# Bias steps as broadcast compares on VectorE, another order of the first operands, and three groups of transposes a chunk later

## The chip, the cores and the metric

The kernel runs on one core of a Trainium2 chip. The metric is the device time of one execution in microseconds (us). The engines are named as in the profile: PE (TensorE: matrix products and transposes), DVE (VectorE), ACT (ScalarE), POOL (GpSimd) and SP (SyncE, which here only issues DMAs).

## The reference

Two transformer blocks are computed one after the other for 256 tokens of width 2048, in float32.

The first block norms x, projects it to 13,712 columns (`proj = h @ w_in`), and runs three branches: A, sparse attention whose keys are the top 64 of an index score, with a learned bias per distance bucket (`bias = rel_table[t5_bucket(pq[:, :, None] - pk)]`); B, causal attention with low-rank q and k and rotary parts; and C, attention to 256 memory tokens (`mkv = rms_norm(mem) @ w_mem_kv`). Each branch's output is multiplied by silu of a z projection, goes through its matrix of `w_branch`, is gated by a sigmoid and added up, and `x = x + merged @ w_out`.

The second block norms this x (h2), projects to 8192 columns, runs a gated recurrence in two directions (its output is ho) and a short convolution, multiplies by `w_out_2`, norms again (h3), and ends with a gated feed-forward layer and a last norm.

## The kernel before, in words

**Tiling.** Each large matrix product is a Job: 512 columns of a weight, all rows of its depth. Its depth is cut into chunks of two tiles of 128 (KG = 2). A chunk's weights come by one DMA on SP (tile raw, 512 KB), ACT rounds them to wh (L277) and DVE takes the rest as wl (L278); the activations exist as such pairs too. `products` (L281) then issues twelve matmuls per chunk, for two token halves t: wh with the high part (L292), wh with the low part (L293), wl with the high part (L295). There are 764 chunks. `drive` (L297) goes through them: loads are issued up to seven chunks ahead, splits up to three ahead (fewer in the first twelve), then the products, the evacuation at a job's end, and one call of `side`.

**Side work.** Everything else is written as Python generators that yield a number of chunks to wait. `side` (L230) moves the urgent ones on each time, and the lanes (constants, bias, C, A, B, recurrence) in their order until the debt of ACT or DVE is above 1.6; each helper (`act`, `tt`, `ts`, ...) adds an estimate of its operation's time to its engine's debt, and each chunk takes a fixed amount off it. So the order on every engine is fixed when the program is built; each engine then works its queue in order and waits by semaphores. `force` (L247) runs side work until an event has come, when an evacuation needs it; no products lie between its rounds.

**Start.** `constants` issues the loads of the identity (on POOL's queue) and of mem's gains vr (on ACT's). `gen_in` loads mem: its first 512 columns in two halves ahead of the first weights. `begin` (L1065) runs some zero matmuls (`warm`), transposes the first tile of mem in two PSUM banks, transposes the gains (`gains0`), writes mem's first pair of columns as memh and meml, splits the first chunk, and writes the second pair.

**Bias.** `gen_bias` builds A's bias by distance: for each of six units u, `steps(u)` writes 0/1 rows stepm (positions compared with thresholds, ptile), eight matmuls with dbt sum the bucket differences, and a copy goes out to DRAM and back in another layout.

**Transposes.** An activation that feeds the next product is transposed on PE and split, by `gen_T`, some chunks after its evacuation: x after w_out and w_out_2 (`x_next`), ho (`g_evac` of block 2), and the q and k parts of B (`gen_B_half`: POOL norms them and applies rotation, tiles uq, bpe, bpt; two chunks or more later PE transposes).

Of the kernel before, what the change touches and what calls it, by code (L numbers as in the profile page):

```python
# [16 lines left out]
P = 128  # L17
# [9 lines left out]
KG = 2  # L27
# [3 lines left out]
WARM = 3  # L31
# [70 lines left out]
class Builder:  # L102
# [151 lines left out]
    def load_to(self, n):  # L254
        while self.nd < min(len(self.chunks), n):
            d = self.nd
            for f in self.pre.get(d, ()):
                f()
            j, _, ks, _, _ = self.chunks[d]
            r = self.praw.tile([P, KG, 512], F32, name="raw")[:, :len(ks), :j.n]  # L260
            w = j.w[ks[0] * P:(ks[-1] + 1) * P, j.n0:j.n0 + j.n].rearrange("(k p) n -> p k n", p=P)
            if d == 0:
                for k in range(len(ks)):
                    self.nc.sync.dma_start(r[:, k], w[:, k])
            else:
                self.nc.sync.dma_start(r, w)
            self.raws[d] = r
            self.nd += 1

    def split_to(self, n):  # L270
        while self.ns < min(len(self.chunks), n):
            j, _, ks, _, _ = self.chunks[self.ns]
            r = self.raws.pop(self.ns)
            wh = self.ph.tile([P, KG, 512], F32R, name="wh")[:, :len(ks), :j.n]
            wl = self.pl.tile([P, KG, 512], F32R, name="wl")[:, :len(ks), :j.n]
            for k in [slice(i, i + 1) for i in range(len(ks))] if self.ns == 0 else [slice(0, len(ks))]:
                self.nc.scalar.activation(wh[:, k], r[:, k], AF.Copy)  # L277
                self.nc.vector.tensor_tensor(wl[:, k], r[:, k], wh[:, k].bitcast(F32), op=ALU.subtract)  # L278
            self.whs[self.ns] = (wh, wl)
            self.ns += 1  # L280
# [46 lines left out]
    def gen_T(self, src, hi, lo, g=None, ev=None, free=(), nk=4, pause=False):  # L327

        banks = []
        for b in range(nk // 2):  # L330
            p = self.ps()
            for jj in range(2):
                for t in range(2):
                    self.tr(p[:, jj * 256 + t * P:jj * 256 + (t + 1) * P], src(t, 2 * b + jj))
            banks.append(p)
        yield 1
        for b, p in enumerate(banks):
            if b and pause:
                yield 1
            if g is None:  # L340
# [107 lines left out]
    def constants(self):  # L448
        nc, I = self.nc, self.I
        self.ident = self.const([P, P], "ident")  # L450
        nc.gpsimd.dma_start(self.ident, I["k_ident"])
        self.vr0 = self.slots.get([P, P], F32, "vr0")
        nc.scalar.dma_start(self.vr0[:16], I["mem_norm_g"][0].rearrange("(k p) -> k p", p=P))
# [140 lines left out]
    def warm(self):  # L594

        z = self.work([P, 512], "warm")
        self.nc.vector.memset(z, 0.0)
        p = self.ps()
        for _ in range(WARM):
            self.nc.tensor.matmul(p[:, :256], z[:, :P], z[:, :256], start=True, stop=True)  # L600
        y = self.work([P, 512], "warm")
        self.act(y[:, :8], z[:, :8], AF.Square)

# [6 lines left out]
    def gen_in(self, src, name, g0, r, hs, ls, at, every):  # L610
# [3 lines left out]
        def load(c):  # L614
            if c == 0 and at < 0:
                for h in range(2):
                    self.nc.sync.dma_start(tiles[0][:, :, h * 256:(h + 1) * 256], src[:, h * 256:(h + 1) * 256].rearrange("(b p) n -> p b n", p=P))
# [88 lines left out]
    def gen_bias(self):  # L706
# [8 lines left out]
        def steps(u):  # L715
# [3 lines left out]
            ms = [sl.get([P, 2, 512], F32R, "stepm") for _ in range(2)]  # L719
            for j in range(4):  # L720
                for i in range(ng):
                    g = 32 * tt + 4 * ((u - 2 * tt) * ng + i) + j
                    self.ts(ms[j // 2][:, j % 2, i * ns:(i + 1) * ns], self.posS[:, :ns], self.ptile[:, g:g + 1], None, ALU.is_le, eng="g")
# [235 lines left out]
    def gen_B_half(self, half, ct, sw, bc):  # L959
# [5 lines left out]
        for i in range(2):  # L965
# [16 lines left out]
            yield 3  # L982
# [69 lines left out]
    def block1(self):  # L1052
# [12 lines left out]
        def begin():  # L1065
            self.warm()
            next(gmem)
            self.gains0()
            next(gmem)
            self.split_to(1)  # L1070
# [188 lines left out]
    def x_next(self, x, cb, ssp, r, store, g, name):  # L1259
# [5 lines left out]
        def later():  # L1265
            yield 1
# [201 lines left out]
    def block2(self):  # L1468
# [45 lines left out]
        def g_evac(hf):  # L1514
            def evac(pts):
# [10 lines left out]
                def later():  # L1526
                    yield 1
# [189 lines left out]
```

## Time and profile before

| What | Value |
|---|---|
| Times of 3 runs | 2268.71, 2270.42 (median), 2270.98 us |
| Profiled execution, its own time | 2268.29 us |
| Its span in the trace | 2266.4 us |
| PE busy | 2243.3 us (99%) |
| Weight loads (PEld) busy | 1877.0 us (83%) |
| DVE busy | 1318.7 us (58%) |
| ACT busy | 1106.0 us (49%) |
| POOL busy | 368.8 us (16%) |
| Chain that ended last | PE 77%, issue 15%, POOL 1%, DMA 1% |
| Mean granted clock of PE | 0.997 |

The share of busy time says which engine the others work for; where time is lost is read from the waits of that engine and from its timeline. The end of a matmul is modelled in the trace, so the distance from one start to another start is the safer measure. A wait is put down to the engine whose semaphore came last.

### The profile page before, as it was taken

The page shows a single profiled execution, that of the slowest core. Times are in us where ns is not written, and L with a number is a line of the kernel's source. Part 1 is how long each engine was busy: PE and PEld are TensorE (multiplying, and loading weights), DVE is VectorE, ACT ScalarE, POOL GpSimd, SP SyncE. Part 2 cuts the span into 40 slices and gives each one's busy share as a digit, 9 for nine tenths or more (in the row PEclk, how much of TensorE's full clock was granted, in tenths as well). Part 3 has the DMA queues.
Part 4 walks back from the last instruction along what each step waited for, and adds up shares of the span by engine and source line. Part 5 has one row for each costly group of instructions (what it writes and reads, how often), then busy time and mean ns, then how long its engine had stood idle before and what let it go on. Part 6 is the DMA issues. An engine that isn't in the chain of part 4 may idle for free.

```text
span 2266.4 us, 27702 instructions
## 1 busy us (share of the span) xinstructions
PE 2243.3 (99%) x10514; PEld 1877.0 (83%) x10514; DVE 1318.7 (58%) x1460; ACT 1106.0 (49%) x1410; POOL 368.8 (16%) x299
## 2 busy tenths in 40 slices
PE   9989999999999999999999999999999999999998
PEld 7878888888888888878888888888888888888886
DVE  5744676655757555555676786555445444544545
ACT  5634545455555544444654655444444433444434
POOL 2093102201405110000363352000000000000001
PEclk9999999999999999999999999999999999999999
DMA  8545555545655556666655555555565566656564
GB/s 278 186 152 183 162 170 181 179 153 173 194 166 177 167 186 187 192 198 202 185 162 164 168 168 158 184 188 186 186 195 190 190 192 202 202 186 194 188 194 140
DMA packets 214933, 413.99 MB, mean 183 GB/s; under 512 B 13538, under 2 KB 20304, under 8 KB 214800
## 3 DMA queue, kind: packets, MB, share of 16 engines
q1 hardware_dynamic: 211936, 405.98, 56.5%
q0 software_dynamic: 2256, 5.19, 0.8%
q8 instruction: 82, 1.34, 0.2%
q10 hardware_dynamic: 608, 1.06, 0.1%
q14 instruction: 51, 0.42, 0.1%
HBM read 408.51 MB, written 3.67 MB: 182 GB/s over the span
## 4 chain that ended last, share of the span: by engine, by line
PE 77%; issue 15%; POOL 1%; DMA 1%; ACT 0%; DVE 0%; ACTq 0%; POOLq 0%; DVEq 0%; SPq 0%
PE acc L292 23%; PE acc L293 23%; PE acc L295 23%; PE sp L157 4%; PE sp L177 2%; DMA xres<-in_x_dram 0%; DMA gf<-in_final_norm_w_dram 0%; POOL x L132 0%; ACT wh L277 0%; POOL ho L132 0%; POOL bpt L132 0%; ACT x L128 0%; POOL bpe L132 0%; DVE wl L278 0%; POOL rs L201 0%
## 5 line engine op out<-in xcount | busy, mean ns | idle before, releaser
L278 DVE TENSOR_TENSOR wl<-raw,wh 128x1024 fp32r<-128x1024 f32 (+4 forms) x765 | 982.2, 1292 | 794.8 <-ACT wh L277 791.8
L277 ACT ACTIVATE wh<-raw 128x1024 fp32r<-128x1024 f32 (+4 forms) x765 | 800.6, 1053 | 868.2 <-PE acc L293 842.3
L292 PE MATMUL acc<-wh,xh 128*128 128x512 f32 (+2 forms) x864 | 341.6, 395 | 0.0
L293 PE MATMUL acc<-wh,xl 128*128 128x512 f32 (+2 forms) x864 | 337.1, 390 | 0.0
L292 PE MATMUL acc<-wh,h3h 128*128 128x512 f32 x704 | 274.8, 390 | 0.0
L293 PE MATMUL acc<-wh,h3l 128*128 128x512 f32 x704 | 273.9, 389 | 0.0
L295 PE MATMUL acc<-wl,xh 128*128 128x512 f32 (+2 forms) x864 | 229.9, 388 | 0.0
L292 PE MATMUL acc<-wh,h2h 128*128 128x512 f32 x512 | 202.2, 395 | 0.0
L293 PE MATMUL acc<-wh,h2l 128*128 128x512 f32 x512 | 199.4, 390 | 0.0
L295 PEld LDWEIGHTS acc<-wl,xh 128*128 128x128 f32 x864 | 162.2, 188 | 32.8
L293 PEld LDWEIGHTS acc<-wh,xl 128*128 128x128 f32 x864 | 163.5, 189 | 31.2
L292 PEld LDWEIGHTS acc<-wh,xh 128*128 128x128 f32 x864 | 163.5, 189 | 30.9
L295 PE MATMUL acc<-wl,h3h 128*128 128x512 f32 x704 | 188.2, 389 | 0.0
L295 PEld LDWEIGHTS acc<-wl,h3h 128*128 128x128 f32 x704 | 132.1, 188 | 27.5
L293 PEld LDWEIGHTS acc<-wh,h3l 128*128 128x128 f32 x704 | 132.2, 188 | 27.2
L292 PEld LDWEIGHTS acc<-wh,h3h 128*128 128x128 f32 x704 | 132.2, 188 | 27.1
L295 PE MATMUL acc<-wl,h2h 128*128 128x512 f32 x512 | 136.9, 389 | 0.0
L292 PE MATMUL acc<-wh,ah 128*128 128x512 f32 x344 | 134.0, 390 | 0.0
L293 PE MATMUL acc<-wh,al 128*128 128x512 f32 x344 | 133.8, 389 | 0.0
L295 PEld LDWEIGHTS acc<-wl,h2h 128*128 128x128 f32 x512 | 96.1, 188 | 20.0
L292 PEld LDWEIGHTS acc<-wh,h2h 128*128 128x128 f32 x512 | 96.2, 188 | 19.0
L293 PEld LDWEIGHTS acc<-wh,h2l 128*128 128x128 f32 x512 | 96.2, 188 | 18.9
(461 smaller groups left out, 2788.7 us busy)
## 6 DMA issues: line engine op xcount, KB each, us to landing
raw<-in_w_in_dram SPq DMA_DIRECT2D x328, 512.0 KB, 3.7
raw<-in_w_gate_up_dram SPq DMA_DIRECT2D x176, 512.0 KB, 3.7
raw<-in_w_down_dram SPq DMA_DIRECT2D x88, 512.0 KB, 3.9
raw<-in_w_out_dram SPq DMA_DIRECT2D x64, 512.0 KB, 4.1
raw<-in_w_branch_dram SPq DMA_DIRECT2D x48, 512.0 KB, 3.9
raw<-in_w_mem_kv_dram SPq DMA_DIRECT2D x31, 512.0 KB, 4.9
raw<-in_w_in_dram SPq DMA_DIRECT2D x8, 464.0 KB, 3.2
raw<-in_w_in_dram SPq DMA_DIRECT2D x8, 448.0 KB, 3.3
```

The source lines that it names most:

```text
L157: self.nc.tensor.matmul(out, lhsT, rhs, start=start, stop=stop)
L177: self.nc.tensor.transpose(out, in_, self.ident if k == P else self.ident[:k, :k])
L277: self.nc.scalar.activation(wh[:, k], r[:, k], AF.Copy)
L278: self.nc.vector.tensor_tensor(wl[:, k], r[:, k], wh[:, k].bitcast(F32), op=ALU.subtract)
L292: self.nc.tensor.matmul(outs[t], a, wh[:, kk], start=first and kk == 0, stop=False)
L293: self.nc.tensor.matmul(outs[t], b, wh[:, kk], start=False, stop=False)
L295: self.nc.tensor.matmul(outs[t], a, wl[:, kk], start=False, stop=last and kk == len(ks) - 1)
```

## The change

- The first operands: the identity is loaded by ACT's queue, vr by SP's, ahead of mem; the second half of mem's first tile is issued behind the first raw tile. There are four warm matmuls in the program in place of three, the gains are transposed first, and conversion of mem and split of the first chunk take turns (`split_first`). These splits now go through the helpers that add to the debt.
- `steps` makes four compares on DVE per unit, each over 512 columns, with positions and thresholds both broadcast, where POOL made 16 or 8 with one threshold each.
- The wait before the transposes is one chunk longer in `x_next` and for ho (`later`), and in `gen_B_half` for q's parts (`yield 4`).

```diff
@@ load_to
                 for k in range(len(ks)):
                     self.nc.sync.dma_start(r[:, k], w[:, k])
+                    if k == 0:
+                        self.second()
@@ new function
+    def split_first(self, k):
+
+        if k == 0:
+            self.whs[0] = (self.ph.tile([P, KG, 512], F32R, name="wh"), self.pl.tile([P, KG, 512], F32R, name="wl"))
+        r, (wh, wl) = self.raws[0], self.whs[0]
+        self.act(wh[:, k], r[:, k])
+        self.tt(wl[:, k], r[:, k], wh[:, k].bitcast(F32), ALU.subtract)
...
@@ gen_T
+            if pause:
+                yield 1
         yield 1
         for b, p in enumerate(banks):
-            if b and pause:
-                yield 1
-            if g is None:
+            if pause and b == 0:
+                for j in range(2):
+                    self.act(hi[:, j, :], p[:, j * 256:(j + 1) * 256], AF.Copy, scale=g(j))
+                    self.stt(lo[:, j, :], p[:, j * 256:(j + 1) * 256], g(j), hi[:, j, :].bitcast(F32), ALU.mult, ALU.subtract)
+                    yield 1
+            elif g is None:
@@ constants
-        nc.gpsimd.dma_start(self.ident, I["k_ident"])
+        nc.scalar.dma_start(self.ident, I["k_ident"])
...
-        nc.scalar.dma_start(self.vr0[:16], I["mem_norm_g"][0].rearrange("(k p) -> k p", p=P))
+        nc.sync.dma_start(self.vr0[:16], I["mem_norm_g"][0].rearrange("(k p) -> k p", p=P))
@@ gen_in
+                half(0)
+                self.second = lambda: half(1)
@@ gen_bias, steps
+            g0 = 32 * tt + 4 * (u - 2 * tt) * ng
+            thr = self.ptile[:, g0:g0 + 4 * ng].rearrange("p (i j) -> p j i", j=4)
+            pos = self.posS[:, :ns].unsqueeze(1).to_broadcast([P, ng, ns])
             for j in range(4):
-                for i in range(ng):
-                    g = 32 * tt + 4 * ((u - 2 * tt) * ng + i) + j
-                    self.ts(ms[j // 2][:, j % 2, i * ns:(i + 1) * ns], self.posS[:, :ns], self.ptile[:, g:g + 1], None, ALU.is_le, eng="g")
+                self.tt(ms[j // 2][:, j % 2, :].rearrange("p (i s) -> p i s", i=ng), pos,
+                        thr[:, j, :].unsqueeze(2).to_broadcast([P, ng, ns]), ALU.is_le)
@@ gen_B_half
             self.tt(pe, pe, tmp, ALU.add, "g")
-            yield 3
+            yield 4
@@ begin
             self.warm()
-            next(gmem)
             self.gains0()
             next(gmem)
-            self.split_to(1)
+            next(gmem)
+            next(gmem)
+            for k in range(KG):
+                next(gmem)
+                self.split_first(k)
@@ x_next, and g_evac of block 2
         def later():
-            yield 1
+            yield 2
```

**The start, on PE.** Before, the gains' transpose (vr) stands behind mem's eight:

```order
L1713 UNCONDITIONAL_BRANCH
L600 MATMUL sp<-warm 128x256 x3
L177 MATMUL sp<-ident,mem_102 128x128 x8
L606 MATMUL sp<-ident,vr_89 128x16
L292 MATMUL acc<-wh,memh_94 128x512
L293 MATMUL acc<-wh,meml_98 128x512
```

Now, in the same place:

```order
L1741 UNCONDITIONAL_BRANCH
L623 MATMUL sp<-warm 128x256 x4
L627 MATMUL sp<-ident,vr_89 128x16
L177 MATMUL sp<-ident,mem_102 128x128 x8
L304 MATMUL acc<-wh,memh_94 128x512
L305 MATMUL acc<-wh,meml_98 128x512
```

The products' order is as before; ahead of them the gains come first, and there is a warm matmul more.

**The bias steps.** Before, POOL's queue in the stretch of the first three units (rs is a power for a norm; ck and cq are branch C's k and q, normed there; biasd is the bias on its way through DRAM):

```order
L201 TENSOR_TENSOR r_83<-rs_t,cneg 128x2
L137 TENSOR_SCALAR stepm<-posS,ptile 128x128 x16
L201 TENSOR_TENSOR rs_1169<-rs_t,cneg 128x4
L132 TENSOR_TENSOR ck_403<-ck_403,rs_1169 128x512 x2
L137 TENSOR_SCALAR stepm<-posS,ptile 128x128 x16
L741 DMA biasd_1128<-bev 128x4x128
L137 TENSOR_SCALAR stepm<-posS,ptile 128x256 x8
L201 TENSOR_TENSOR rs_1382<-rs_t,cneg 128x4
L132 TENSOR_TENSOR cq_1287<-cq_1287,rs_1382 128x512 x2
```

Now DVE's queue in the same stretch, between the splits wl (bev is the copy of a unit's sums, ss a sum of squares):

```order
L290 TENSOR_TENSOR wl<-raw,wh 128x1024
L132 TENSOR_TENSOR stepm<-posS,ptile 128x512 x4
L290 TENSOR_TENSOR wl<-raw,wh 128x1024 x2
L146 TENSOR_REDUCE ss_705<-sq 128x2
L290 TENSOR_TENSOR wl<-raw,wh 128x1024
L137 TENSOR_SCALAR rs_t<-ss_705 128x4
L290 TENSOR_TENSOR wl<-raw,wh 128x1024
L137 TENSOR_SCALAR cq_1236<-acc,r_83 128x512
L132 TENSOR_TENSOR stepm<-posS,ptile 128x512 x4
L290 TENSOR_TENSOR wl<-raw,wh 128x1024 x2
L153 COPY bev<-sp 128x512
```

All six steps are gone from POOL; on DVE a split stands behind each group of four. Four or five splits lie from one group to the next.

**The end of branch B, on PE.** Before, a whole chunk lies between the last four transposes of prob and the six matmuls that use them and others (ukv holds B's values; the row with x6 holds two matmuls of one round and four of the next):

```order
L295 MATMUL acc<-wl,xh_110 128x512 x4
L157 MATMUL sp<-ukv_5142,pT 128x128 x4
L177 MATMUL sp<-ident,prob 128x128 x4
L292 MATMUL acc<-wh,xh_111 128x512
L293 MATMUL acc<-wh,xl_115 128x512
...
L295 MATMUL acc<-wl,xh_111 128x512 x4
L157 MATMUL sp<-ukv_5165,pT 128x128 x6
```

Now the last products ahead of them, and what follows:

```order
L305 MATMUL acc<-wh,xl_114 128x512
L307 MATMUL acc<-wl,xh_110 128x512 x4
L157 MATMUL sp<-ukv_5096,pT 128x128 x4
L177 MATMUL sp<-ident,prob 128x128 x4
L157 MATMUL sp<-ukv_5126,pT 128x128 x6
L304 MATMUL acc<-wh,xh_107 128x512
```

The transposes have moved next to the six matmuls, all of it in the forced rounds ahead of the evacuation of B's first z.

## Rows read from the trace of the kernel before

**Rows 1.** Waits of PE, then of its loads: us in total, times, longest.

```profile
PE sp L177 <- POOL cq L132: 3.1, 2, 2.4
PE sp L157 <- POOL stepm L137: 2.6, 2, 1.6
PE sp L177 <- POOL bpe L132: 1.7, 1, 1.7
PE acc L292 <- ACT wh L277: 1.7, 1, 1.7
...
PE sp L177 <- DVE x L132: 1.3, 3, 0.7
...
PEld sp L177 <- DVE x L132: 3.2, 6, 1.2
...
PEld sp L177 <- POOL ho L132: 0.7, 1, 0.7
```

**Rows 2.** Timeline of PE, 119 to 130: start, us, what.

```profile
118.97 0.39 PE L292 MATMUL acc<-wh,xh 128*128 128x512 f32 x1
...
119.88 1.08 PE L295 MATMUL acc<-wl,xh 128*128 128x512 f32 x4
...
129.20 1.09 PE L295 MATMUL acc<-wl,xh 128*128 128x512 f32 x4
```

**Rows 3.** Timeline of PE, 150 to 161.

```profile
151.04 1.07 PE L295 MATMUL acc<-wl,xh 128*128 128x512 f32 x4
...
159.76 1.09 PE L295 MATMUL acc<-wl,xh 128*128 128x512 f32 x4
```

**Rows 4.** Busy times in a stretch; PEclk is the granted clock.

```profile
125.50:128.50 3.00, 3.00 (x8) 2.32 (x8) 0.69 (x1) 0.00 (x0) 2.92 (x4) 0.50 0.04 14
```

**Rows 5.** Timelines of DVE and POOL, 126 to 160.

```profile
142.96 0.16 DVE L137 TENSOR_SCALAR rs_t<-ss 128x4 f32<-128x4 f32 x1
...
139.40 12.23 POOL L137 TENSOR_SCALAR stepm<-posS,ptile 128x256 fp32r<-128x256 f32 x8
151.60 1.03 POOL L201 TENSOR_TENSOR rs<-rs_t,cneg 128x4 f32<-128x4 f32 x1
152.71 2.74 POOL L132 TENSOR_TENSOR cq<-cq,rs 128x512 f32<-128x512 f32 x2
```

**Rows 6.** Timeline of PE around undisturbed transposes of mem, and the first of x.

```profile
25.45 1.07 PE L295 MATMUL acc<-wl,memh 128*128 128x512 f32 x4
...
27.16 0.47 PE L292 MATMUL acc<-wh,memh 128*128 128x512 f32 x1
...
968.87 1.07 PE L295 MATMUL acc<-wl,mgh 128*128 128x512 f32 x4
...
972.01 0.48 PE L292 MATMUL acc<-wh,mgh 128*128 128x512 f32 x1
```

**Rows 7.** DVE groups by shape: busy us, mean ns, idle before.

```profile
L278 DVE TENSOR_TENSOR wl<-raw,wh 128x1024 fp32r<-128x1024 f32 x52 | 64.5, 1246 | 43.3 <-ACT wh L277 42.6 <-PE acc L293 0.3 <-PE sp L177 0.2
...
L132 DVE TENSOR_TENSOR ctmp<-posS,k 128x256 f32<-128x256 f32 x1 | 0.4, 419 | 0.0
...
L132 DVE TENSOR_TENSOR nkb<-hK,nkb 128x1024 f32<-128x1024 f32 x2 | 6.2, 3092 | 0.0
```

**Rows 8.** Timeline of ACT at the end of branch B.

```profile
783.69 0.58 ACT L128 ACTIVATE pT<-sp 128x512 f32<-128x512 f32 x1
```

**Rows 9.** Timeline of PE at the start.

```profile
1.48 2.93 PE L600 MATMUL sp<-warm 128*128 128x256 f32 x6 [1.48 <-DVE warm L597]
...
9.15 0.79 PE L292 MATMUL acc<-wh,memh 128*128 128x512 f32 x1 [1.66 <-ACT wh L277]
...
12.73 1.12 PE L295 MATMUL acc<-wl,memh 128*128 128x512 f32 x4
```

**Rows 10.** DMA issues in the first 16 us: KB each, median us to landing.

```profile
mem<-in_mem_dram SPq DMA_DIRECT2D x2, 256.0 KB, 3.4
...
vr<-in_mem_norm_g_dram ACTq DMA_DIRECT2D x1, 8.0 KB, 2.5
```

More of the change, by code (lines that the diff above doesn't have):

```diff
@@ L30 @@
 NSLOT = 31
-WARM = 3
+WARM = 4
 T2 = 5
@@ L268, in load_to @@
             self.nd += 1
+    def split_first(self, k):
[4 more added lines that the diff above has]
+        self.tt(wl[:, k], r[:, k], wh[:, k].bitcast(F32), ALU.subtract)
+        if k == KG - 1:
+            del self.raws[0]
+            self.ns = 1
     def split_to(self, n):
@@ L275, in split_to @@
             wl = self.pl.tile([P, KG, 512], F32R, name="wl")[:, :len(ks), :j.n]
-            for k in [slice(i, i + 1) for i in range(len(ks))] if self.ns == 0 else [slice(0, len(ks))]:
-                self.nc.scalar.activation(wh[:, k], r[:, k], AF.Copy)
-                self.nc.vector.tensor_tensor(wl[:, k], r[:, k], wh[:, k].bitcast(F32), op=ALU.subtract)
+            self.nc.scalar.activation(wh, r, AF.Copy)
+            self.nc.vector.tensor_tensor(wl, r, wh.bitcast(F32), op=ALU.subtract)
             self.whs[self.ns] = (wh, wl)
@@ L597, in warm, with busy @@
         self.nc.vector.memset(z, 0.0)
-        p = self.ps()
-        for _ in range(WARM):
-            self.nc.tensor.matmul(p[:, :256], z[:, :P], z[:, :256], start=True, stop=True)
+        self.zero = z
+        self.busy(WARM)
         y = self.work([P, 512], "warm")
         self.act(y[:, :8], z[:, :8], AF.Square)
+    def busy(self, n):
+        p = self.ps()
+        for _ in range(n):
+            self.nc.tensor.matmul(p[:, :256], self.zero[:, :P], self.zero[:, :256], start=True, stop=True)
     def gains0(self):
@@ L615, in load @@
             if c == 0 and at < 0:
-                for h in range(2):
-                    self.nc.sync.dma_start(tiles[0][:, :, h * 256:(h + 1) * 256], src[:, h * 256:(h + 1) * 256].rearrange("(b p) n -> p b n", p=P))
+                half = lambda h: self.nc.sync.dma_start(tiles[0][:, :, h * 256:(h + 1) * 256],
+                                                        src[:, h * 256:(h + 1) * 256].rearrange("(b p) n -> p b n", p=P))
+                half(0)
+                self.second = lambda: half(1)
                 self.done(f"{name}L{c}")
@@ L1526, in later @@
                 def later():
-                    yield 1
+                    yield 2
                     yield from self.gen_T(lambda t, j: o[:, t, j * P:(j + 1) * P], h, l, g=lambda j: self.vT[:, c + j:c + j + 1],
```

## The prediction

> **What bounds the kernel now.** I read the busy table first, the one that stands in the section on the profile: TensorE (PE) is busy for 99% of the span, so only what makes PE stand still, or run slowly, can move the time. So I took the list of PE's waits next. Five of its eight entries make 10.4 us, and each is at a place that this diff touches [rows 1]. Their true cost is larger than the list says, since a matmul's end is modelled and since a stop lowers the clock, so I measured each in the timeline of PE, as the distance between two rows against what the work between them takes undisturbed. Products of 512 columns stand 0.227 us apart: from 118.97 to 119.88 there are four [rows 2]. Four products and eight transposes behind them, up to the next chunk, take 27.16 - 25.45 = 1.71 us, so eight transposes are 0.80 [rows 6]. A chunk is twelve products, 2.72 us; its weights are split on ScalarE and DVE up to three chunks ahead.
>
> **Bias steps from GpSimd to VectorE.** Before, POOL computes 64 step rows. Between the last products of two chunks at 119.88 and 129.20 lie twelve products and eight stepm matmuls, 20 x 0.227 = 4.54 us, and 9.32 are spent: 4.78 lost, partly in waits for POOL's stepm, partly because the granted clock in 125.5 to 128.5 is 0.50, the 1.2 GHz level, after PE had stood [rows 2, 4]. The stop at cq is of the same origin: VectorE (DVE) has written the sums at 142.96, but POOL is in a run of eight compares of 12.23 us until 151.60; only then come the power (1.03) and the two products (2.74) for which PE's transposes wait [rows 5]. From 151.04 to 159.76 are 8.72 us against 2.72 + 0.80 = 3.52: 5.20 lost [rows 3]. Without compares POOL can start 8.5 us earlier, and the wait of cq is 3.1: this stop goes whole.
>
> What is added are 24 tensor_tensor on DVE, 128x512, in six steps of four. The trace has no compare of two tensors on DVE. A 128x256 product with a broadcast operand takes 0.419, so two are 0.84; half a split of 128x1024 is 0.62; and the worst product in SBUF of the whole run, nkb, took 3.09 for 1024, 1.55 per 512 [rows 7]. I take 0.70, near the first two: 2.8 us per step and 16.8 in all. PE needs a step four or more chunks (10.9 us) after it is issued, so the matmuls find it done. What stands behind the compares on DVE are the splits (wl) that PE needs; they run three chunks ahead, 8.2 us, and a step with one split takes 2.8 + 1.25 = 4.05 [rows 7]. Cost on PE: nothing, and if that cover were gone, up to the 16.8. I count 4.8 + 5.2 = 10.0 gained.
>
> The planner counts the compares as DVE work and holds branch C back for them, by some ten chunks in the order; C is still done when z of c asks for it, and no row of PE is moved next to one that it waits for, so this is counted at nothing.
>
> **One chunk later.** The stop at bpe is 1.7 [rows 1]; the chunk added (2.72 x 384 / 512 = 2.0 for the narrower products there) is longer, so it goes: 1.7. The transposes of x after w_out wait for DVE's add, which itself waited for the residual's load. The first lost 972.01 - 968.87 = 3.14 against 1.71, so 1.43 [rows 6]. For all x and ho the list of weight loads says 3.2 + 0.7 = 3.9, as an upper bound; the 1.43 alone is the lower one. I take 3.0, nearer to the loads' list, because it counts more places than the first. What is late next: h2's and h3's last group is ready two chunks into a job that first uses it in its seventh chunk, so nobody.
>
> The same delay has a price at the end of branch B. There the evacuation of z forces B to its end, with no products between. Before, four transposes of prob had a whole chunk of cover before their copy was used; now they stand directly ahead of the six pT matmuls, four of which need ScalarE's copy of them. That copy took 0.58 [rows 8]; a little for the handover is added and the two matmuls that don't need it are taken off. Bounds: 0 if records pipeline well, 3.2 if PE stands 1.5 and loses the clock as in rows 2 (eight products at twice 0.227 cost another 1.8, less what overlaps). Taken: 0.6 lost.
>
> **The start.** PE's warm matmuls begin at 1.48 and six took 2.93; then it waits for the identity that POOL's queue loads, transposes at half rate, waits again (1.66) for the first split, and begins products at 9.15 [rows 9]. Eight products then take 12.73 - 9.15 = 3.58 us, 0.45 each, the 1.2 GHz level, before it runs at 0.227. In the new order the identity goes out on ScalarE's queue, where the 8 KB gains took 2.5 us from issue to landing, and the gains on SP ahead of the first half of mem (256 KB, 3.4) [rows 10]. The row of warm matmuls gets two instructions longer and, at 0.45 each, ends at about 1.48 + 8 x 0.45 = 5.1; the identity (0.72 + 2.5, with a margin for eight times the bytes) is there by then. The first half of mem, issued half a microsecond later than now, lands at about 1.2 + 3.4 = 4.6; four transposes (0.80, twice what four take at full rate) behind the gains' end at 6.1. The second half of mem now stands behind a raw block: issued near 2.2, it lands 3.4 to 4.2 later, up to 6.4, and its transposes end by 7.2, while ScalarE converts and splits the first k. First product at about 7.3: 1.85 earlier, bounds 0 (all loads later) and 2.5. As PE now works from 1.48 almost without a gap, the clock should rise before the products, which is worth 3.58 - 8 x 0.227 = 1.76 more; against this, the second block's conversion and split on ScalarE and DVE will be asked for earlier than they can be, which I estimate at 1 us. Together 1.85 + 1.76 - 1.1 = 2.5, bounds 0 and 3.6.
>
> The Trainium skill (TensorE: Matmul & The Clock Gate, Part 4: PE-mode transpose) speaks against the clock's share: it says that transposes do not count as busy time for the clock gate. By this rule the transposes between the warm matmuls and the products would leave the clock low, which is the first rival below. The trace of before cannot decide it, as its transposes there have stops on both sides.
>
> **Sum.** 10.0 + 1.7 + 3.0 - 0.6 + 2.5 = 16.6 us. The profiled execution took 2268.29, so 2251.7 for such a one; its time lies 2.1 us below the median 2270.42 of the timed runs, so I forecast 2270.4 - 16.6 = 2253.8.
>
> **Rivals.**
> *The clock stays low through the first products* (the transposes don't raise it). For it: after six warm matmuls and eight transposes the products of before still began at half rate; against it: PE stood still twice in between, which it would not now. The 1.76 goes, and of the 1.1 against it only about 0.85 stays, since loads of the second block are then asked for later: the start gives 1.85 - 0.85 = 1.0 in place of 2.5: 2255.3. 20%.
> *The forced end of B costs the clock too*: the order stands for it, the smallness of a 0.58 copy against it. 3.2 in place of 0.6: 2256.4. 8%.
> *Compares as slow as nkb*, 1.55 each: a step is 6.2, and in the five chunks (13.6 us) between steps stand five splits (6.2) and some 2.5 of other work: 14.9, so 1.3 late each time, 7.8 for six steps: 2261.6. For it: nkb has SBUF on both sides like the compares; against it: the other rows of this shape are at 0.42 per 256. 8%.
> *Slower: the step holds back the splits until PE stops and the clock falls.* Place: each of the six steps on DVE. Price: 4.78 as in rows 2, six times 28.7: 2253.8 + 28.7 = 2282.5. It decides from the point where a step and a split exceed the 8.2 us of lead, that is compares above (8.2 - 1.25) / 4 = 1.7 us, above the worst row. 4%.
> That the change doesn't do what it says (cq's wait stays, since its sums come late): 5.2 less, 2259.0, 3%; POOL's 8.5 us of slack speak against it.
>
> **Numbers.** The forecast has 57%, with its own range 2250 to 2258. 2248 to 2264 takes in all rivals but the slow one and the bounds of start and transposes. About 0.2% (4.5 us) can be told from no change; faster than 2265.9 are all cases but the slower one and the bad side of the slow compares: faster 0.91, same 0.05, slower 0.04.
>
> **What would show it.** PE's list of waits has no stepm, no cq, no bpe, and x and ho far below 3.9; no stretch at 0.50 near 125 or 156; DVE has 24 compares of about 0.70 and POOL none; the first product at 7.3 and the ninth under 10; a stop of about 0.6 behind B's last transposes. I am wrong if PE waits for wl between 100 and 210 us, or if the compares take 1.5.

## The result, and the profile after

The changed kernel takes 2251.74 us (median of 4 runs, 2251.58 to 2252.52) against 2270.7 for the kernel before beside it (4 runs, 2268.71 to 2271.57): ratio 0.9918, 95% interval [0.9901, 0.9936]. It is faster by 19.0 us by the medians. The two profiled executions differ by 16.4 us of span (2266.4 and 2250.0), and the stretches below account for 16.3 of them. The other 2.6 lie between the profiles and the medians: the timed runs of before scatter over 3 us, and its profiled one (2268.29) is among its quicker ones. One place where executions with the old delays differ is shown under the bias steps; how much of the 2.6 it makes is not shown.

TensorE's waits, to be read beside [rows 1] (us in total, times, longest):

```profile
PE sp L623 <- DVE warm L614: 1.5, 1, 1.5
PE sp L177 <- DMA mem<-in_mem_dram: 0.7, 1, 0.7
PE acc L304 <- ACT wh L128: 0.7, 1, 0.7
PE sp L157 <- ACT pT L128: 0.2, 1, 0.2
```

No cq, stepm, bpe, x or ho is left. The first three entries lie in the first ten microseconds, the last is the new one at the end of branch B. Busy times by stretch, where [rows 2 to 4] had their stops and the half clock (after the stretch its length, then busy time of PE, PEld, DVE, ACT and POOL, the granted clock, the DMA share and GB/s):

```profile
110.00:120.00 10.00, 10.00 (x46) 8.29 (x45) 9.81 (x17) 4.76 (x5) 0.00 (x0) 1.00 0.60 187
120.00:130.00 10.00, 10.00 (x46) 8.23 (x45) 8.69 (x12) 3.76 (x4) 3.96 (x3) 1.00 0.65 210
150.00:160.00 10.00, 10.00 (x45) 8.26 (x44) 8.61 (x10) 4.17 (x6) 4.52 (x3) 1.00 0.66 217
```

PE is busy throughout at clock 1.00; the price stands in the third engine column, VectorE, busy for 8.6 to 9.8 of 10 us. The compares themselves (count; ns shortest, median, longest; us of the first and last start):

```profile
L132 DVE TENSOR_TENSOR stepm<-posS,ptile x24: 677/684/1556, 115.5 to 187.9; 128x512 fp32r<-128x512 f32 x24
```

The start, beside [rows 9]:

```profile
1.49 3.78 PE L623 MATMUL sp<-warm 128*128 128x256 f32 x8 [1.49 <-DVE warm L614]
5.20 0.28 PE L627 MATMUL sp<-ident,vr 16*128 16x16 f32 x1
5.62 0.66 PE L177 MATMUL sp<-ident,mem 128*128 128x128 f32 x4
7.00 0.65 PE L177 MATMUL sp<-ident,mem 128*128 128x128 f32 x4 [0.73 <-DMA mem<-in_mem_dram]
7.41 0.47 PE L304 MATMUL acc<-wh,memh 128*128 128x512 f32 x1
7.73 0.39 PE L305 MATMUL acc<-wh,meml 128*128 128x512 f32 x1
...
9.26 0.50 PE L304 MATMUL acc<-wh,memh 128*128 128x512 f32 x1 [0.68 <-ACT wh L128]
...
10.29 1.08 PE L307 MATMUL acc<-wl,memh 128*128 128x512 f32 x4
```

To see where the time came from, I compare the start of the first product with each activation in both traces (mem is the first job, x the next, uc stands behind branch C, l, in the trace lk, behind the bpe transposes, ub behind branch B, the end is PE's last matmul). Each stretch holds the same matmuls before and after, but for two warm ones more at the start. From uc to lq both take 166.05 us.

| stretch | before, us | after, us | gained |
|---|---|---|---|
| start to first x | 104.46 | 102.49 | 1.97 |
| first x to first uc (stepm, cq) | 288.83 | 278.90 | 9.93 |
| lq to l (bpe) | 20.18 | 18.21 | 1.97 |
| l to ub (branch B's end) | 253.32 | 254.23 | -0.90 |
| ub to PE's end (x, ho) | 1423.81 | 1420.49 | 3.32 |
| all | 2256.65 | 2240.37 | 16.29 |

### The profile page after: what moved, and what is told of

The parts are those of the page before. It is cut to its first block, busy times and chain, and to the rows that moved or that the text cites. A ratio compares the mean times of both kernels' runs of the same rounds, so it can differ in the third digit from the quotient of the medians.

```text
span 2250.0 us, 27646 instructions
## 1 busy us (share of the span) xinstructions
PE 2237.0 (99%) x10516; PEld 1873.7 (83%) x10516; DVE 1331.0 (59%) x1484; ACT 1105.9 (49%) x1410; POOL 303.5 (13%) x234
## 4 chain that ended last, share of the span: by engine, by line
PE 98%; ACT 0%; DMA 0%; DVE 0%; issue 0%; POOL 0%; SPq 0%; ACTq 0%; POOLq 0%; DVEq 0%
PE acc L304 31%; PE acc L305 30%; PE acc L307 30%; PE sp L157 4%; PE sp L177 3%; DMA raw<-in_w_mem_kv_dram 0%; POOL x L132 0%; ACT x L128 0%; ACT sq L128 0%; DVE x L132 0%; DVE wl L290 0%; DVE ss L146 0%; SPq L637 0%; DVE ukv L137 0%; DVE x L141 0%
## 5 line engine op out<-in xcount | busy, mean ns | idle before, releaser
L290 DVE TENSOR_TENSOR wl<-raw,wh 128x1024 fp32r<-128x1024 f32 (+1 forms) x763 | 974.5, 1286 | 773.8 <-ACT wh L289 771.2
L289 ACT ACTIVATE wh<-raw 128x1024 fp32r<-128x1024 f32 (+1 forms) x763 | 799.2, 1055 | 857.2 <-PE acc L305 832.8
```

The costliest lines, as they stand in the source:

```text
L289: self.nc.scalar.activation(wh, r, AF.Copy)
L290: self.nc.vector.tensor_tensor(wl, r, wh.bitcast(F32), op=ALU.subtract)
```

## The experiments

Each was timed beside the kernel before, the last two once only; the verdicts below also rest on the profile of each, by the same stretches. Three dots in a diff stand for lines or arguments left out.

### One part at a time

**Bias steps only.** The kernel before, with `steps` of the changed one:

```diff
...
-                for i in range(ng):
-                    g = 32 * tt + 4 * ((u - 2 * tt) * ng + i) + j
-                    self.ts(..., self.posS[:, :ns], self.ptile[:, g:g + 1], None, ALU.is_le, eng="g")
+                self.tt(..., pos, thr[:, j, :].unsqueeze(2).to_broadcast([P, ng, ns]), ALU.is_le)
```

> The kernel before with one part of the change: the compares of the bias steps on VectorE, broadcast, four per unit. Theory (the two stops at 121 to 129 and 151 to 160 us both come from GpSimd's compares): the list of PE's waits loses stepm and cq, no stretch near 125 or 156 runs at a granted clock of 0.50, and the span falls by 9.9 us against the profiled 2266.4 (4.8 + 5.2 of the prediction). Rival (cq's stop has another origin, its sums come late): only stepm goes, 4.8. Rival (this part alone makes the difference between the profiled gain of 16.4 and the timed one of 19.0): the time falls by 12 or more.

Measured: 2258.94 us, before 2269.36, ratio 0.9953 [0.994, 0.9967]. The waits for stepm and cq are gone, and from x to uc it takes 278.83 us, 10.00 less than before. The one edit removes both stops, also the one at cq, whose operands it does not touch: cq had stood behind the compares on POOL. The median is 10.4 lower, but the span of the profile, 2260.2, only 6.2 and not the 9.9 that I expected: in this execution the first product with x comes 0.69 later than in the profile of before, and from ub to the end of PE it takes 3.05 more. Most of that is the first stop at x, which this edit does not touch:

```profile
959.56 1.07 PE L295 MATMUL acc<-wl,mgh 128*128 128x512 f32 x4
962.90 2.35 PE L177 MATMUL sp<-ident,x 128*128 128x128 f32 x8 [2.27 <-DVE x L132]
964.91 0.78 PE L292 MATMUL acc<-wh,mgh 128*128 128x512 f32 x1
```

From 959.56 to 964.91 are 5.35 us against 1.71 of work, so 3.64 are lost where [rows 6] lose 1.43. VectorE's add waited 5.52 us for the residual's load here, and 3.98 in before's profile. So the stop at x, which the longer delay removes, differs in size from one execution to the next.

**The start only.** The changed kernel with the old compares and the old delays.

```diff
...
-                self.tt(..., pos, thr[:, j, :].unsqueeze(2).to_broadcast([P, ng, ns]), ALU.is_le)
+                for i in range(ng):
...
+                    self.ts(..., self.posS[:, :ns], self.ptile[:, g:g + 1], None, ALU.is_le, eng="g")
...
-            yield 4
+            yield 3
...
-            yield 2
+            yield 1
...
```

> The kernel before with only the new order of the first operands and the fourth warm matmul. Theory: the first product comes at 7.4 in place of 9.15, at full rate, and the first product with x 2.0 us earlier; the span falls by 2.0, and the stops at stepm and cq stay. Rival (what is won at the start is lost to the next wait, which stays where a load sets it): under 0.5.

Measured: 2271.17 us, ratio 1.0004 [0.9995, 1.0013]: nothing. My theory of 2.0 less fell. Its waits (before: stepm 2.6):

```profile
PE sp L157 <- POOL stepm L137: 3.8, 2, 2.7
PE sp L177 <- POOL cq L132: 3.1, 2, 2.4
```

The first product with x comes 1.91 us earlier than before, that with uc 0.38 later. PE waits longer for the first step, and the granted clock from 120 to 130 us is 0.77, where it was 0.83. POOL's first step in the kernel before, in this one, and in the next one, which has the delays only:

```profile
111.02 14.15 POOL L137 TENSOR_SCALAR stepm<-posS,ptile 128x128 fp32r<-128x128 f32 x16 [14.50 <-ACT sq L128]
```

```profile
113.42 14.33 POOL L137 TENSOR_SCALAR stepm<-posS,ptile 128x128 fp32r<-128x128 f32 x16 [16.08 <-DVE ptile L137]
```

```profile
111.98 14.15 POOL L137 TENSOR_SCALAR stepm<-posS,ptile 128x128 fp32r<-128x128 f32 x16 [14.50 <-ACT sq L128]
```

While PE comes 1.91 earlier, POOL starts its compares 2.40 later, because VectorE writes the thresholds ptile later: the rows of constants ahead of them in its queue (cos to rsk, 100.55 to 103.04 before) now stand behind the evacuation of cv (102.76), which came after them before (104.66). At cq POOL's power starts at 151.93 against 151.60. The stops alone would not have eaten the gain: with the delays only, the order up to uc is that of before, the first product with x happens to come 0.96 later, POOL's compares start 0.96 later, and uc comes 0.94 later, so that a shift of the start passes both stops whole. So what cost the gain is the new order of the side work. That the first splits, which now count in the planner's debt, have moved it is my reading of the change; no run separates it. In the changed kernel the same later order costs nothing, since the compares have left POOL.

**The delays only.** The kernel before with `yield 4` in `gen_B_half` and `yield 2` in both `later`:

```diff
-            yield 3
+            yield 4
...
-            yield 1
+            yield 2
...
```

> The kernel before with only the three waits before transposes one chunk longer (x, ho, and q's parts in branch B). Theory: bpe gives 2.0, x and ho 3.3, and the forced end of branch B costs 0.6 to 0.9: the span falls by 4.4 to 4.7, and PE waits some 0.5 behind the last transposes of prob. Rival (the forced end costs the clock as well): a stretch at a granted clock of 0.50 behind 770 us, and the span falls by 2 to 3.

Measured: 2263.55 us, ratio 0.9975 [0.9965, 0.9984]. lq to l gains 1.97, and from uc to PE's end it takes 4.39 us less than before, the same as in the changed kernel (4.39). The span falls by 3.4 only, as the first product with x came 0.96 later in this profile; the median falls by 5.8. PE waits 0.2 behind the last transposes of prob, not the 0.5 expected. So by the profiles the terms are 1.97, 9.93 to 10.00 and 4.39, and in the changed kernel they add; the start alone gave nothing.

### What the compares may cost on VectorE

**Not counted.** The changed kernel, with the compares kept out of the planner's debt:

```diff
-                self.tt(ms[j // 2]..., pos, thr..., ALU.is_le)
+                nc.vector.tensor_tensor(ms[j // 2]..., pos, thr..., op=ALU.is_le)
```

> The changed kernel with the compares on VectorE as they are, but left out of the planner's count of VectorE's work, so that branch C and the index work are not held back for them. Theory (the compares are covered by the lead of the splits, wherever they stand): time as the changed kernel's, within 1 us. Rival (the planner's room for them is what keeps PE from waiting): stops of PE at wl, stepm or C's transposes between 100 and 210 us, 2 to 8 us slower than the changed kernel.

Measured: 2256.18 us, ratio 0.994 [0.9928, 0.9953], 4.4 above the changed kernel. My theory fell and the rival held, by a stop of C's transposes; there is a new wait, `PE sp L177 <- POOL ck L132: 2.0, 2, 1.4`. POOL and DVE in this kernel (start, us, engine):

```profile
119.99 6.59 POOL L201 TENSOR_TENSOR rs<-rs_t,cneg 128x4 f32<-128x4 f32 x1 [22.64 <-DVE rs_t L137]
126.67 2.04 POOL L132 TENSOR_TENSOR ck<-ck,rs 128x512 f32<-128x512 f32 x2
```

```profile
119.75 0.16 DVE L137 TENSOR_SCALAR rs_t<-ss 128x4 f32<-128x4 f32 x1
119.82 2.35 DVE L290 TENSOR_TENSOR wl<-raw,wh 128x1024 fp32r<-128x1024 f32 x2
122.09 2.49 DVE L747 TENSOR_TENSOR stepm<-posS,ptile 128x512 fp32r<-128x512 f32 x4
124.50 1.22 DVE L290 TENSOR_TENSOR wl<-raw,wh 128x1024 fp32r<-128x1024 f32 x1
```

The sums rs_t are in time, at 119.91, even earlier than the changed kernel's 122.09. What is late is POOL's power on 4 columns, 6.59 us where it took 1.03 in [rows 5]: it ends 0.9 us after the last of seven DVE instructions that each read two tensors of SBUF and follow one another without a gap. The Trainium skill (SBUF — State Buffer, Who interferes with whom) says that such a VectorE instruction and a GpSimd instruction that reads SBUF exclude each other, the later waiting for the whole of the earlier. The trace agrees on the exclusion. By the rule the power would wait for one instruction, and so it mostly is (122.17 in the changed kernel: 1.92 us, the end again 0.9 after that of one split); here it did not get its turn at any of the six handovers within the seven. What decides when it does stays open.

**The same, with one operand each.** Four compares of 128 columns, or two of 256, against one threshold per partition, again not counted:

```diff
...
+                for i in range(ng):
+                    g = g0 + 4 * i + j
+                    nc.vector.tensor_scalar(ms[j // 2][:, j % 2, i * ns:(i + 1) * ns], self.posS[:, :ns], self.ptile[:, g:g + 1], None, op0=ALU.is_le)
```

> The kernel whose comparisons on VectorE are not counted by the planner (2256.18, with a stop at ck of 2.0 us), but with each comparison of 512 columns written as four of 128 (or two of 256) that compare the positions with one threshold per partition, so that they read one tensor of SBUF instead of two. In the uncounted kernel GpSimd's power for ck's norm ran from 119.99 to 126.59, 6.59 us against 1.03 where VectorE does nothing, while VectorE issued splits and comparisons without a gap from 119.82 to 125.7. Theory (GpSimd is held as long as VectorE goes from one instruction with two SBUF inputs to the next, and gets its turn when one without them comes): the small comparisons let it in at about 122.1, so the power takes 2 to 4 us, ck's products end by 126.3 and the stop at ck falls from 2.0 to under 0.6; VectorE's own time per unit becomes 2.5 to 4 us (16 of 0.16 to 0.25), and the time is 2252 to 2254. Rival (ck is late because of the planner's order and the queue on VectorE, whatever the operands): the stop stays at 1.5 us or more, 2255.5 to 2257. Rival on the other side (64 small instructions cost VectorE so much that splits come late): new waits for wl, above 2257.

Measured: 2253.42 us, ratio 0.9931 [0.9918, 0.9943], 2.8 less than with two operands. No wait for ck is left, only one of 0.6 for cq. POOL, then DVE:

```profile
121.11 3.08 POOL L201 TENSOR_TENSOR rs<-rs_t,cneg 128x4 f32<-128x4 f32 x1 [23.37 <-DVE rs_t L137]
124.27 2.23 POOL L132 TENSOR_TENSOR ck<-ck,rs 128x512 f32<-128x512 f32 x2
```

```profile
120.94 2.36 DVE L290 TENSOR_TENSOR wl<-raw,wh 128x1024 fp32r<-128x1024 f32 x2
123.21 4.94 DVE L749 TENSOR_SCALAR stepm<-posS,ptile 128x128 fp32r<-128x128 f32 x16
```

The power again ends 0.9 us after a two-operand instruction (121.11 + 3.08 = 124.19 against 123.30), which is now the second wl: it got in where the compares begin, and not behind them. The rows on DVE are slowed too while POOL works (16 in 4.94 us, where 12 took 2.44 at 116.79), so with the single operand the two still hold each other up; in this kernel POOL got in earlier. Of the 1.7 that it takes more than the changed kernel, 0.86 lie between x and uc (279.76 us) and 0.48 ahead of x (102.97), where its clock rose late (see the start, below). The stop at ck is thus POOL's waiting for VectorE, and not a late rs_t; that the number of operands decides the turn is supported by these two kernels and not proved.

**One operand, counted.**

```diff
...
+                    self.ts(ms[j // 2][:, j % 2, i * ns:(i + 1) * ns], self.posS[:, :ns], self.ptile[:, g:g + 1], None, ALU.is_le)
```

> The changed kernel (comparisons counted) with the same comparisons against one threshold per partition, 64 in place of 24. Theory (TensorE has no stop in this stretch in the changed kernel, so freeing GpSimd sooner can give nothing): the time stays within 0.8 us of 2251.74, while no instruction on VectorE takes 1.5 us beside ck's and cq's products on GpSimd any longer. Rival (the small ones are dearer, and the planner counts 0.08 us for each of them, so that side work moves later): 1 to 6 us more, with stops behind 200 us as in the kernel that issues the comparisons twice.

Measured: 2252.29 us, ratio 0.9925 [0.9912, 0.9939], within 0.6 of the changed kernel: where PE has no stop, freeing POOL gives nothing. The longest compare is still 1.08 us, so this part of the expectation was only half right.

**Compares twice.**

```diff
-            for j in range(4):
+            for j in (0, 0, 1, 1, 2, 2, 3, 3):
```

> The changed kernel, but every comparison for the bias steps is issued twice (the second writes the same values): 24 more of 0.684 us on VectorE, 16.4 us between 115 and 190 us, which is what a comparison of 1.37 us instead of 0.68 would add. VectorE is busy for 61.4 of the 80 us from 110 to 190 in the changed kernel, so 18.6 are idle. Theory (the comparisons are free only because VectorE has idle time beside products, and the splits' wl queue behind them): the idle time is almost used up and the queue ahead of a split grows by up to 2.7 us per unit, so some waits for wl or ck appear between 112 and 130, where VectorE was busy for 18.5 of 20 us: 2 to 8 us more, 2254 to 2260. Rival (the planner counts the comparisons, puts side work later, and so hides all of it): within 1 us of 2251.74 and no wait of TensorE above 0.5 us there.

Measured: 2263.6 us, ratio 0.997 [0.996, 0.9981]: 11.9 above the changed kernel, more than I expected, and elsewhere. Stretches of this kernel, with the columns as above:

```profile
120.00:140.00 20.00, 20.00 (x89) 16.52 (x88) 19.79 (x23) 7.27 (x8) 5.47 (x4) 1.00 0.55 173
330.00:350.00 20.00, 13.49 (x61) 10.85 (x60) 16.78 (x49) 7.13 (x11) 5.93 (x6) 0.86 0.23 64
```

```profile
PE sp L177 <- POOL akav L132: 3.5, 2, 3.2
PE sp L157 <- DVE pTl L132: 3.0, 2, 1.8
```

From 120 to 140 VectorE is full and PE loses nothing. But the planner, counting the work, puts side work later: the two pTl of C's attention, at 332.73 and 336.22, then stand on VectorE in a long row of small selection instructions (MAX8 and MATCH_REPLACE8, 0.3 to 0.4 us each), and PE has no product between the matmuls that wait for them. The longest stop, 3.2, is behind them, at 346.07: the sums that POOL needs for akav, A's keys and values, leave VectorE at the end of the same row, at 343.83. In the changed kernel PE waits for neither. So the bill comes 150 us later. That it is the counting which moves the side work, and not the time on VectorE, is argued: no kernel issues the compares twice uncounted.

### The end of branch B, and the start

**B's tail**, with the second group of probability transposes one call earlier:

```diff
-            yield 4
+            yield 4 if half == 0 else 3
```

> The changed kernel, but the second group of B's probability transposes comes three calls after its scores instead of four, so that one chunk of products stands again between those transposes and the six pT matmuls. The changed kernel stops there for 0.46 us (773.02) and 0.16 us (773.53), and the step from the first product of l to that of ub came out 0.90 us longer than in the kernel before. Theory (the forced end of B is a real cost of the change and its stop is all of it): both stops go, the first product of ub comes 0.6 to 0.9 us earlier against l, the time is 2250.8 to 2251.2 us. Rival 1 (the added step is the ukv wait of 0.28 us and chance): l to ub changes by under 0.3 us and the time stays at 2251.4 to 2252.1. Rival 2 (one call less puts the transposes before the softmax is done): a new wait of TensorE for prob of 0.5 us or more, 2252.3 or later.

Measured: 2251.95 us, ratio 0.9918 [0.9904, 0.9932]: no difference from the changed kernel, where I expected 0.6 to 0.9 less. The stops at pT are gone, and l to ub takes 253.93 us, 0.30 less than in the changed kernel and 0.61 more than before. So the forced end costs 0.3, not 0.9. The rest is another wait, which was not there before; in the changed kernel's PE row and its list of weight loads it reads

```profile
571.36 0.39 PE L305 MATMUL acc<-wh,lk 128*128 128x512 f32 x1
571.85 0.50 PE L304 MATMUL acc<-wh,lk 128*128 128x512 f32 x1
572.19 0.39 PE L305 MATMUL acc<-wh,lk 128*128 128x512 f32 x1
```

```profile
PEld acc L304 <- DVE ukv L137: 0.5, 1, 0.5
```

Spacings of 0.49 and 0.34 in place of 0.23 make 0.4: with the bpe stop gone, PE is earlier at the next accumulator than VectorE has emptied it. Some 0.2 remain unassigned.

**The gains on ScalarE's queue**, mem's first half first on SP:

```diff
-        nc.sync.dma_start(self.vr0[:16], ...)
+        nc.scalar.dma_start(self.vr0[:16], ...)
```

> The changed kernel, but the small load of mem_norm_g is issued by ScalarE behind ident, so that the first half of mem is the first that SyncE issues. In the changed kernel that half is issued at 1.19 us and lands at 5.57, 4.4 us later; in the kernel before it was issued at 0.73 and landed at 3.7, 3 us later. Theory (the small load ahead of it costs the issue slot of 0.45 us and part of the longer flight): the half lands at 4.2 to 5.1, the first product with mem starts 0.4 to 0.7 us earlier than 7.41 unless raw's first block (landed 6.23) holds it, and raw's second block (8.55) comes 0.4 us earlier; the time is 0.3 to 0.7 us less, 2251.0 to 2251.4. Rival (the first product waits for raw's first block and its split, not for mem): the product comes within 0.2 us of 7.41 and the time stays within 0.3 us of 2251.74. Rival on the other side (vr behind ident lands later than mem, and its transposes wait): vT late, the first product 0.3 us or more later.

Measured: 2251.83 us, ratio 0.9919 [0.9906, 0.9932]: no difference from the changed kernel. The half lands at 4.05 instead of 5.57 and the first product comes at 6.84 instead of 7.41, but chance can be most of this: with the gains ahead of it the half landed between 4.34 and 5.57 in the other profiles, and in the next kernel, which has the same start as this one, the first product came at 7.62.

**Both:**

> The changed kernel with both edits, the second group of B's transposes one call earlier and mem_norm_g issued by ScalarE. Theory (both are real and lie far apart, 8 and 773 us): the sum of the two alone, 0.9 to 1.6 us less than the changed kernel, 2250.1 to 2250.8. Rival (what is gained at the start is given back at the next wait, as it was when only the start was changed): no more than the 0.6 to 0.9 us of the tail, 2250.8 to 2251.2.

Measured: 2251.54 us, ratio 0.9917 [0.9904, 0.993], 0.4 us of span less than the changed kernel. The 0.9 to 1.6 that I expected did not come. It has the lowest median of the study, but 0.2 us lies within the runs' scatter: no version beats the changed kernel by an amount that can be told.

**Do transposes raise the clock?** In the control the four warm matmuls read ident as weights, so that they wait for it; in the other kernel sixteen transposes of zeros take their place.

```diff
-            self.nc.tensor.matmul(p[:, :256], self.zero[:, :P], self.zero[:, :256], start=True, stop=True)
+            self.nc.tensor.matmul(p[:, :256], self.ident, self.zero[:, :256], start=True, stop=True)
```

```diff
-        for _ in range(n):
-            self.nc.tensor.matmul(p[:, :256], self.zero[:, :P], self.zero[:, :256], start=True, stop=True)
+        for _ in range(4 * n):
+            self.nc.tensor.transpose(p[:, :P], self.zero[:, :P], self.ident)
```

> The changed kernel, but its four warm matmuls read ident as weights instead of zeros, so that they start when ident lands (2.6 us in the changed kernel) and not at 1.49. They are the control for the next kernel: same columns, matmuls. Theory: they run from about 2.7 to 6.5 at 0.47 us each pass as before, the transposes of mem come behind them, and the first products of mem run at a spacing of 0.227 us; the first product comes 0.5 to 1.5 us later than 7.41. Rival (the warm matmuls have to begin by 1.5 us for the clock to be up): the first products are spaced by 0.45 us.

> The changed kernel, but the four warm matmuls (128x256, fp32, two passes each) are replaced by sixteen transposes of a zeroed 128x128 fp32 tile through ident, which start when ident lands, as the control's matmuls do; nothing but transposes then stands ahead of the first products. Theory (these transposes raise the granted clock as matmuls do): the transposes quicken from about 0.24 us to 0.11 us on their way, or the first products of mem have a spacing of 0.227 us at once, as in the control. Rival (the rule of the Trainium skill, page 'TensorE: Matmul & The Clock Gate', Part 4: a transpose does not raise the clock): all transposes stay at the low rate and the first products have a spacing of 0.45 us or so for a few us before they quicken, so the product after the first chunk comes 1.5 to 3 us later than in the control.

Measured: 2252.07 and 2252.33 us. In the control the first products stand 0.23 us apart from 8.37 on, as expected, so the warm matmuls need not begin at 1.49. PE in the kernel whose warming is all transposes:

```profile
2.80 3.65 PE L623 MATMUL sp<-ident,warm 128*128 128x128 f32 x16 [2.80 <-DMA ident<-in_k_ident_dram]
6.38 0.28 PE L627 MATMUL sp<-ident,vr 16*128 16x16 f32 x1
6.59 1.42 PE L177 MATMUL sp<-ident,mem 128*128 128x128 f32 x8
8.65 0.50 PE L304 MATMUL acc<-wh,memh 128*128 128x512 f32 x1 [0.64 <-ACT wh L128]
8.99 0.40 PE L305 MATMUL acc<-wh,meml 128*128 128x512 f32 x1
9.22 0.39 PE L304 MATMUL acc<-wh,memh 128*128 128x512 f32 x1
```

and the transposes of mem in it (count; ns shortest, median, longest), those that touch 6.0 to 7.2 us, then those that touch 7.4 to 8.0 (one is in both):

```profile
L177 PE MATMUL sp<-ident,mem x3: 391/421/474, 6.6 to 7.1; 128*128 128x128 f32 x3
```

```profile
L177 PE MATMUL sp<-ident,mem x6: 272/273/391, 7.1 to 7.7; 128*128 128x128 f32 x6
```

The sixteen start 0.21 us apart (2.80 to 6.02); among mem's eight, at about 7.3, the spacing falls to 0.11, and the products, the first matmuls with weights in this kernel, start 0.23 apart once the first is through. So with fp32 transposes alone ahead of them the products ran at the upper level. The level is read from the spacing, since the profile's column of the granted clock reads 1.00 from 0 to 16 us, in the slow stretch too; the trace's first record of that clock, at the upper level, begins at 7.30 us here, among the transposes. The rule of the Trainium skill (TensorE: Matmul & The Clock Gate, Part 4: PE-mode transpose), which gives its figures for bf16, does not hold for these transposes.

## Why the prediction was right, point by point

The forecast was 2253.8 with 2248 to 2264; the time is 2251.74. In the profiled executions the sum was 16.6 and the measured one 16.3. It is nearer than its parts: bpe, x and ho came out 0.6 above the forecast together, the start 0.5 and the end of B 0.3 below it, and these errors cancel.

- **Bias steps and cq: 10.0 forecast, 9.93 measured.** One cause for both stops, as [rows 5] had it; the bias-only kernel shows it.
- **Compares: 0.70 forecast, 0.684 median.** Three of the 24 took 1.5 us, because POOL multiplied ck or cq beside them; their sum is 18.95 us in place of 16.8, all covered. The timeline of DVE has such a row at 125.20, where one of the four is the long one, beside POOL's products:

```profile
125.20 3.36 DVE L132 TENSOR_TENSOR stepm<-posS,ptile 128x512 fp32r<-128x512 f32 x4
```

```profile
124.17 2.04 POOL L132 TENSOR_TENSOR ck<-ck,rs 128x512 f32<-128x512 f32 x2
```

- **The price of the rival "as slow as nkb" was misread.** nkb's 3.09 us [rows 7] is no speed of that operation. In the changed kernel it stands beside POOL's nfb and ends 1.1 us after it; the split ahead of it, usually 1.2, takes the same 3.42 and ends 1.1 after POOL's nkf (DVE, then POOL):

```profile
1087.01 3.42 DVE L290 TENSOR_TENSOR wl<-raw,wh 128x1024 fp32r<-128x1024 f32 x1
1090.35 3.42 DVE L132 TENSOR_TENSOR nkb<-hK,nkb 128x1024 f32<-128x1024 f32 x1
```

```profile
1085.97 3.38 POOL L132 TENSOR_TENSOR nkf<-hQ,nkf 128x1024 f32<-128x1024 f32 x1
1089.31 3.37 POOL L132 TENSOR_TENSOR nfb<-hK,nfb 128x1024 f32<-128x1024 f32 x1
```

- **"The planner holds branch C back; counted at nothing"** was right as a sum, but the reason given left out what the counting is worth: without it, splits and compares close up on VectorE and keep POOL out, and the time is 4.4 us longer.
- **If the cover were gone, "up to the 16.8".** With twice the compares it was 11.9, by side work that came late at 333 to 346 us and not by the splits, which the prediction had named.
- **One chunk later: bpe 1.7 forecast, 1.97 measured** (0.4 of it given back at ukv); **x and ho 3.0, measured 3.32; B's end -0.6, measured -0.90** by the stretch, of which the tail itself is 0.3, so that term is near for the wrong reason: the wait at ukv was not foreseen. The stop behind B's last transposes is there, smaller than forecast. The 3.9 that the prediction calls an upper bound for x and ho is none: in the profile of the bias-only kernel ub to PE's end takes 6.37 more than in the changed one.
- **The start: 2.5 forecast, 1.97 measured.** First product 7.41 against 7.3; in this profile the clock was up by then. (The prediction estimates 1 us for the loads of the second block and takes 1.1 off; with 1 the term is 2.6.) In this profile the loads were late: mem's first half took 4.4 us to land, not 3.4, and raw's second block landed at 8.55, so that the ninth product came at 10.29 and not under 10. The gain is 1.74 at the first product, 2.44 at the ninth and 1.97 at the first x. Over the profiles of the study, the first x starts at 104.46, 105.15 and 105.42 with the old first operands and at 102.09 to 102.97 in nine with the new ones (the two with the gains on ScalarE's queue among them): by the means 2.4, so the 2.5 was well sized.
- **The clock at the start did not always rise in time.** In one of these nine, the kernel with one operand uncounted, the eight products of the first chunk ran 0.45 us apart on average, as in the kernel before, and the trace's first record of the upper level is at 10.99 us, where the changed kernel has it at 5.64:

```profile
7.67 0.80 PE L304 MATMUL acc<-wh,memh 128*128 128x512 f32 x1
8.27 0.63 PE L305 MATMUL acc<-wh,meml 128*128 128x512 f32 x1
...
11.27 1.09 PE L307 MATMUL acc<-wl,memh 128*128 128x512 f32 x4
```

  Its warm matmuls and gains started at the same times as in the changed kernel; why the clock rose later is not shown. Its first x came at 102.97, 0.4 behind the mean of the other eight. So the first rival's state occurs, but its price here was 0.4 and not the 1.5 that the prediction gave it, and its reason, that transposes do not raise the clock, is refuted by the kernel with transposes only.
- **The other cases.** That B's end costs 3.2, that cq's wait stays and that splits stop PE were all refuted by the rows after. The forecast lies 2.1 above the measured median, since I moved the profiled execution's sum to the median shown: from the profiled 2268.29 the same sum gives 2251.7. By the medians the parts came out larger, the bias steps alone 10.4 and the delays alone 5.8, and the stop at x above, 1.43 in one profile and 3.64 in another, is one place where that can come from.

## What to carry to other kernels

Work moved off a slow engine is free where a faster one has idle time at that place, but look at both engines' timelines: an instruction on VectorE with two operands in SBUF and one on GpSimd hold each other up, and a close row of the first kept a tiny one of the second out for 6.6 us here. Parts of a change need not add: the start alone gave nothing, since with it the order had moved what a later stop waited for, and the shift of the start itself would have passed. Where the order changes, the price can show far from the edit, so compare landmarks over the whole run. And a stop read in one profile can be larger in the next execution, so a sum of stops belongs to the execution that it was read from.

## What was not expected of the hardware

- GpSimd's power on 4 columns took 1.03 us at 125.14 in the kernel before, with VectorE idle. Where it starts beside a two-operand instruction on VectorE it ends 0.9 us after the end of one: mostly the first (1.7 to 2.1 us), in two places the second (3.08 and 3.06, both with one operand uncounted), in one the seventh (6.59).
- Landings at the start scatter between executions: mem's first half, issued at 1.19, was there 3.2 to 4.4 us later, and the changed kernel's profile has the slowest.
- A first product that starts 0.96 us later (8.37, in the control of the transposes) made the first x only 0.23 later. In the changed kernel the fifth product had waited 0.68 us for the split of raw's second block, and at the ninth (10.54 against 10.29) only 0.25 of the difference was left.
